# A hybrid attention, recurrence and expert-retrieval block on one core: fewer candidate sums, a gate product shared by two engines, another load order and five score blocks held

## The chip, the cores and the metric

The kernel runs on one core of one Trainium2 chip. The metric is the device time of one execution in microseconds. The time before is the median of three runs, 3784.94 us (3783.61 to 3789.96).

## The reference

One layer over 512 tokens of width 2048. A mixer (forgetting attention with 8 heads beside an RWKV-7 recurrence with 16 heads) is followed by a channel part that retrieves single-neuron experts. A vector `c` modulates both:

```python
mod = silu(c) @ w_ada + b_ada                     # 2048 -> 6 x 2048
h   = rms_norm(x, norm_mix_w) * (1 + sc1) + sh1
x   = x + g1 * (concat(fox(h @ w_in), rwkv(h @ w_in)) @ w_out)
h2  = rms_norm(x, norm_ffn_w) * (1 + sc2) + sh2
# product-key retrieval, 8 heads, 128 x 128 keys, 16384 experts
q = (h2 @ w_query).reshape(T, 8, 2, 128)
s = einsum('thpd,hpkd->thpk', q, sub_keys)
top_s, top_i = top_k(s, 16)                       # per head and key half
cand_s = top_s[:, :, 0, :, None] + top_s[:, :, 1, None, :]   # 16 x 16 sums
best_s, best_pos = top_k(cand_s, 16)
gates = softmax(best_s)
# experts: sum_e gate_e * v_e * gelu(u_e . h2)
x = x + g2 * ffn
```

Both top-16 lists are sorted. A sum of place a in the first and place b in the second list can be among the 16 largest only if (a + 1)(b + 1) is at most 16.

## The kernel before

Activations lie with the model dimension on the partitions, 16 tiles of 128 by 512 tokens. Weights and activations are split into a high and a low part (`split_raw`, L100 and on: ScalarE casts the high part at L103, VectorE or GpSimd subtracts for the low one at L106), and each product is three matmuls (`mm3`, L110 to L112). `Stream` loads weights in halves of 512 KB, splits three halves ahead (`SPLIT`) and hands them to TensorE in one order for the whole kernel.

**Modulation and first projections** (L279 to L385). For the first two of the six modulation vectors, eight rounds of 4 MB of `w_ada` are loaded by `ada_load` (L293) in eight tiles of two rows of blocks each; a tile tag holds `WB` = 11 buffers. In `ada_part` (L300) VectorE multiplies and adds the first eight blocks (`KD`) into two accumulators, while TensorE sums the other eight with `on_pe` in two halves of 256 columns that share one PSUM area, `psx`; VectorE adds each half to an accumulator before the next may be written. `ada_sum` then totals over the partitions, `ada_mod` adds the bias, `first_h` scales two tiles of `x`, and `strm.outer` runs the first seven projections over them on TensorE. The order on VectorE and TensorE is written out by hand here, and three steps of the next round's `ada_part` stand ahead of `ada_mod`.

**Mixer** and its output projection follow, and after them the second norm. They are planned by `Clock`, a small planner in the kernel: each generator yields the TensorE time that it takes and the time after which it is due again, and the planner picks what is emitted next. Outside the parts ordered by hand a scheduler of the framework may still move instructions of an engine.

**Routing** (`route`, L1056). The sixteen query projections `wq` are followed by scores against 128 sub-keys (L1068). For each of four tiles of tokens VectorE takes the 16 largest of 128 (L1073 to L1078: maximum of eight, index search, replacement, maximum, index search). After the second half of a head it builds the 256 sums of a tile with one addition (`cd`, L1088), takes their 16 largest in the same five passes (L1091 to L1096), and finds the two key indices by comparing the high and the low four bits of the position with 0 to 15 (`eq`, L1112; L1123). GpSimd does the low-part subtractions of `wq` meanwhile.

**Gates** (`gates`, L1131). For 320 of the 512 tokens the gates become a dense 128 x 128 matrix a token: a one-hot vector of the first key (`oa`) against one of the second key times the gate (`ob`), multiplied on TensorE (L1186), four tokens a group, eight groups a block of 32 tokens. `oa` is built by VectorE in every second group, by GpSimd (L1164) or ScalarE (L1167, L1168) in the others; `ob` always by VectorE, in four comparisons with a multiplication in the same instruction (L1172). ScalarE copies the result to `gst` (L1188), and each block of 32 tokens is stored to DRAM (`g_d`). Two groups are built ahead, in three buffers.

**Experts.** `scores(e)` (L1038) computes a block of 128 experts for the 320 tokens: 48 matmuls and a Gelu. The first `NB` = 11 blocks are computed ahead of the last stage; `fill2` emits the last `LAST` = 3 of them after the gates. The last stage reads the gates back (`gt`, L1276), weighs the activations (L1278), splits them (L1284, L1285) and combines them with `v`, while the other 192 tokens gather their experts' rows by indirect DMA.

Of the kernel before, what the change touches and what calls it, by code (L numbers as in the profile page):

```python
# [18 lines left out]
P = 128  # L19
# [12 lines left out]
def block_kernel(ctx: ExitStack, tc: tile.TileContext, I: dict, O: dict, dbg=None):  # L32
# [223 lines left out]
    LAST = 3  # L256
# [22 lines left out]
    with ExitStack() as x0:  # L279
        x0.enter_context(tc.manual_schedule(engines={mybir.EngineType.DVE, mybir.EngineType.PE}))  # L280
        p0 = x0.enter_context(tc.tile_pool(name="ph0", bufs=1, reuse_waits="tile"))
        KD, WB = 8, 11
# [10 lines left out]
        def ada_load(jj):  # L293
            w = []
            for a in (4, 5, 6, 7, 0, 1, 2, 3):
                w.append(p0.tile([P, 2, T], F32, tag="wada", name=f"wada{jj}{a}", bufs=WB))
                nc.sync.dma_start(w[-1], I["wada"][jj, :, a * 2:(a + 1) * 2, :])
            return w[4:] + w[:4]

        def ada_part(jj, w, acc):  # L300
# [9 lines left out]
            for k in range(KD):  # L310
                a, wk = acc[k % 2], w[k // 2][:, k % 2, :]
                if k == 3:
                    on_pe(hs[0])
# [4 lines left out]
                if k in (4, 7):  # L318
                    c_ = hs[k // 6]
                    V.tensor_tensor(acc[1][:, c_], acc[1][:, c_], psx, op=ALU.add)  # L320
                    if k == 4:
                        on_pe(hs[1])
                yield
            V.tensor_tensor(acc[0], acc[0], acc[1], op=ALU.add)

# [32 lines left out]
        for k in range(NK):  # L358
            x = xs[k] if k < 2 else p0.tile([P, T], F32, tag=("prd", "acc2")[k % 2], name=f"n1sq{k}", bufs=2)
# [684 lines left out]
    with ExitStack() as rx:  # L1044
# [11 lines left out]
        def route(n, pj, tops):  # L1056
# [8 lines left out]
            yield 0.0, 1.0  # L1065
# [6 lines left out]
            for t in range(NT):  # L1072
                V.max(tv[:, p_, t, 0:8], sc[:, t, :])  # L1073
                V.max_index(ti[:, p_, t, 0:8], tv[:, p_, t, 0:8], sc[:, t, :])
                s2 = px.tile([P, 256], F32, tag="s2", name=f"s2{n}{t}", bufs=2)
                V.match_replace(s2[:, :P], tv[:, p_, t, 0:8], sc[:, t, :], NEG)
                V.max(tv[:, p_, t, 8:16], s2[:, :P])
                V.max_index(ti[:, p_, t, 8:16], tv[:, p_, t, 8:16], s2[:, :P])  # L1078
# [6 lines left out]
            bi = px.tile([P, 3, NT, 16], U32, tag="bi", name=f"bi{h}", bufs=2)  # L1085
            for t in range(NT):
                cd = px.tile([P, 16, 16], F32, tag="cd", name=f"cd{h}{t}", bufs=2)
                V.tensor_tensor(cd, tv[:, 0, t, :, None].to_broadcast([P, 16, 16]),  # L1088
                                tv[:, 1, t, None, :].to_broadcast([P, 16, 16]), op=ALU.add)
                cf = cd.rearrange("p a b -> p (a b)")  # L1090
                V.max(bv[:, t, 0:8], cf)  # L1091
                V.max_index(bi[:, 0, t, 0:8], bv[:, t, 0:8], cf)
                s2 = px.tile([P, 256], F32, tag="s2", name=f"c2{h}{t}", bufs=2)
                V.match_replace(s2, bv[:, t, 0:8], cf, NEG)
                V.max(bv[:, t, 8:16], s2)
                V.max_index(bi[:, 0, t, 8:16], bv[:, t, 8:16], s2)  # L1096
                yield 0.0, ck.dve(2.05)
# [340 lines left out]
```

## Time and profile before

| | |
|---|---|
| median of three runs | 3784.94 us |
| the profiled execution | 3788.3 us |
| its span, first to last instruction | 3786.6 us |
| TensorE busy | 3525.6 us, 93% |
| VectorE busy | 3065.7 us, 81% |
| ScalarE busy | 1247.1 us, 33% |
| GpSimd busy | 1101.4 us, 29% |
| mean granted TensorE clock | 0.962 |

Busy shares over the whole span mix stages with different limits. The stages can be told apart by line: modulation up to some 157 us, mixer and output projection to 1490, second norm and first query projections to 1598, routing to 1823, gates to 1941, the wait for the gates' way through DRAM to 1967, experts to the end. In a timeline the first column is the start, the second the time that the listed instructions last; the distance from one start to the next is the step, which is shorter than the duration where instructions overlap.

### The profile page before, as it was taken

The page shows a single profiled execution, that of the slowest core. Times are in us where ns is not written, and L with a number is a line of the kernel's source. Part 1 is how long each engine was busy: PE and PEld are TensorE (multiplying, and loading weights), DVE is VectorE, ACT ScalarE, POOL GpSimd, SP SyncE. Part 2 cuts the span into 40 slices and gives each one's busy share as a digit, 9 for nine tenths or more (in the row PEclk, how much of TensorE's full clock was granted, in tenths as well). Part 3 has the DMA queues.
Part 4 walks back from the last instruction along what each step waited for, and adds up shares of the span by engine and source line. Part 5 has one row for each costly group of instructions (what it writes and reads, how often), then busy time and mean ns, then how long its engine had stood idle before and what let it go on. Part 6 is the DMA issues. An engine that isn't in the chain of part 4 may idle for free.

```text
span 3786.6 us, 55808 instructions
## 1 busy us (share of the span) xinstructions
PE 3525.6 (93%) x21269; PEld 3127.3 (83%) x21269; DVE 3065.7 (81%) x5314; ACT 1247.1 (33%) x1807; POOL 1101.4 (29%) x692
## 2 busy tenths in 40 slices
PE   6888989999899999998969999999999999999999
PEld 4666766766667778777869999999999999999999
DVE  5687677786875564599978989898989989999996
ACT  3332322423323321323643333333333333333332
POOL 3310110100100000431333444444434444444540
PEclk9888989999989998999989999999999999999999
DMA  8633342433433565222469999999999999999996
GB/s 336 220 105 94 107 119 67 135 93 99 114 113 106 172 211 174 80 81 84 170 247 355 393 384 380 386 389 393 392 379 391 395 383 382 383 387 390 392 386 224
DMA packets 317821, 955.43 MB, mean 252 GB/s; under 512 B 77161, under 2 KB 121449, under 8 KB 266609
## 3 DMA queue, kind: packets, MB, share of 16 engines
q1 hardware_dynamic: 210416, 541.84, 40.0%
q0 software_dynamic: 55296, 402.68, 26.6%
q10 hardware_dynamic: 51840, 7.35, 1.3%
q8 instruction: 167, 2.74, 0.3%
q14 instruction: 102, 0.83, 0.1%
HBM read 916.32 MB, written 35.41 MB: 251 GB/s over the span
## 4 chain that ended last, share of the span: by engine, by line
PE 54%; DVE 16%; DMA 6%; issue 3%; ACT 2%; POOL 0%; ACTq 0%; SPq 0%; DVEq 0%; POOLq 0%
PE po L112 8%; PE po L111 7%; PE po L110 7%; DMA wadl<-wada 3%; DVE rows L1262 2%; DMA u_0raw<-uT 1%; DVE accl L413 1%; DVE ob L1172 1%; PE gp L1186 1%; DVE hl L1285 1%; DVE h2t L1270 1%; DVE pr L636 1%; DVE eq L1112 1%; DVE cd L1088 1%; ACT u_0h L103 1%
## 5 line engine op out<-in xcount | busy, mean ns | idle before, releaser
L1251 POOL DMA_INDIRECT rows<-vn,idx x192 | 401.1, 2089 | 459.5 <-DVE h2t L1270 428.5
L1251 POOL DMA_INDIRECT rows<-un,idx x192 | 363.2, 1892 | 538.9 <-DVE rows L1262 520.3
L1270 DVE SCALAR_TENSOR_TENSOR h2t<-rows,gat,h2t 128x2048 f32<-128x2048 f32 x190 | 445.8, 2346 | 1.3
L1262 DVE SCALAR_TENSOR_TENSOR rows<-rows,h2t 128x2048 f32<-128x2048 f32 x192 | 435.8, 2284 | 0.0
L413 DVE SCALAR_TENSOR_TENSOR accl<-wadl,c,accl 128x256 f32<-128x256 f32 x480 | 245.4, 511 | 106.0 <-DMA wadl<-wada 96.8
L103 ACT CAST u_1h<-u_1raw 128x1024 fp32r<-128x1024 f32 x128 | 134.6, 1051 | 333.2 <-PE po L111 265.0
L103 ACT CAST u_0h<-u_0raw 128x1024 fp32r<-128x1024 f32 x128 | 134.4, 1050 | 297.7 <-DMA u_0raw<-uT 19.0
L1296 DVE TENSOR_TENSOR acc<-acc,po 128x320 f32<-128x320 f32 x240 | 115.5, 481 | 63.5 <-PE po L112 63.4
L106 DVE TENSOR_TENSOR u_1l<-u_1raw,u_1h 128x1024 fp32r<-128x1024 f32 x128 | 155.9, 1218 | 6.6 <-ACT u_1h L103 6.6
L106 DVE TENSOR_TENSOR u_0l<-u_0raw,u_0h 128x1024 fp32r<-128x1024 f32 x128 | 155.9, 1218 | 0.0
L1278 DVE TENSOR_TENSOR at<-at,gt 128x320 f32<-128x320 f32 x128 | 62.1, 489 | 94.1 <-ACT at L1041 83.9
L756 DVE SCALAR_TENSOR_TENSOR st<-st,pend,pu 64x64 f32<-64x64 f32 x240 | 67.0, 279 | 62.8 <-PE pu L752 58.7
L636 DVE TENSOR_TENSOR pr<-zz,msys 128x16 f32<-128x16 f32 (+30 forms) x248 | 105.9, 427 | 3.9
L106 POOL TENSOR_TENSOR wq_0l<-wq_0raw,wq_0h 128x1024 fp32r<-128x1024 f32 x13 | 33.9, 2606 | 241.7 <-ACT wq_0h L103 241.7
L1186 PE MATMUL gp<-ob,oa 128*128 128x128 f32 x640 | 83.9, 281 | 15.8 <-ACT oa L1168 14.3
L1164 POOL TENSOR_SCALAR oa<-iota,selT 128x128 f32<-128x128 f32 x80 | 61.6, 785 | 126.5 <-ACT selT L1150 73.5
L1186 PEld LDWEIGHTS gp<-ob,oa 128*128 128x128 f32 x640 | 77.3, 191 | 21.3 <-ACT oa L1168 16.5
L1172 DVE TENSOR_SCALAR ob<-iota,selT 128x128 f32<-128x128 f32 x320 | 89.2, 346 | 0.0
L743 POOL MEMSET st<- 64x64 f32 x16 | 2.3, 146 | 253.9 <-DVE st L756 253.9
L638 DVE TENSOR_REDUCE zz<-pr 128x8 f32<-128x16 f32 (+30 forms) x248 | 71.4, 288 | 2.5
L103 ACT CAST wF_0h<-wF_0raw 128x1024 fp32r<-128x1024 f32 x32 | 33.6, 1049 | 97.7 <-PE wF43ps L111 13.3
L740 DVE TENSOR_TENSOR uh<-uh,pw 32x128 f32<-32x128 f32 x120 | 34.1, 284 | 37.4 <-PE pw L739 34.8
(4432 smaller groups left out, 12463.9 us busy)
## 6 DMA issues: line engine op xcount, KB each, us to landing
wadl<-wada SPq DMA_DIRECT2D x256, 256.0 KB, 3.0
u_0raw<-uT SPq DMA_DIRECT2D x128, 512.0 KB, 10.0
u_1raw<-uT SPq DMA_DIRECT2D x128, 512.0 KB, 9.7
wada<-wada SPq DMA_DIRECT2D x64, 512.0 KB, 9.0
gt<-g_d SPq DMA_DIRECT2D x32, 640.0 KB, 14.4
g_d<-gst SPq DMA_DIRECT2D x10, 1920.0 KB, 6.6
wF_0raw<-win SPq DMA_DIRECT2D x32, 512.0 KB, 3.8
wF_1raw<-win SPq DMA_DIRECT2D x32, 512.0 KB, 3.6
```

The lines of the kernel that those rows point to most:

```text
L103: S.copy(wh, raw)
L106: eng.tensor_tensor(wl, raw, wh.bitcast(F32), op=ALU.subtract)
L110: PE.matmul(ps, ah, bh, start=first, stop=False)
L111: PE.matmul(ps, ah, bl, start=False, stop=False)
L112: PE.matmul(ps, al, bh, start=False, stop=last)
L413: V.scalar_tensor_tensor(acc, w[:, k, :], c16[:, a + k:a + k + 1], acc, op0=ALU.mult, op1=ALU.add)
L636: V.tensor_tensor(pr[:, :, :m], zz[:, s_:, :].rearrange("p t j -> p j t"), msys[:, s_:s_ + 1, s_:].to_broadcast([P, 8, m]), op=ALU.mult)
L1172: V.tensor_scalar(ob[:, u, :], iota, selT[:, 1, t0 + u:t0 + u + 1], selT[:, 2, t0 + u:t0 + u + 1], op0=ALU.is_equal, op1=ALU.mult)
L1186: PE.matmul(b0.rearrange("p (j t) -> p t j", t=4)[:, u, :], oa[:, u, :], ob[:, u, :], start=True, stop=True)
L1251: G.indirect_dma_start(out=b_, out_offset=None, in_=I["vn" if side else "un"], in_offset=bass.IndirectOffsetOnAxis(ap=idx[i][:, c_:c_ + 1] ...
L1262: V.scalar_tensor_tensor(b_, b_, 1.0, h, op0=ALU.mult, op1=ALU.mult, accum_out=dot[i][:, c_:c_ + 1])
L1270: V.scalar_tensor_tensor(h, b_, g[:, c_:c_ + 1], h, op0=ALU.mult, op1=ALU.add)
```

## The change

The routing builds 112 sums a head and tile: the first four places of the first list with all sixteen of the second (64 sums), and places 4 to 15 with the first four of the second (48 sums), with two additions for all four tiles. Passes are 112 wide. The position is decoded for both parts and joined with three more operations; the tiles for it have one buffer. The gates build `ob` in five of eight groups with one two-input comparison on VectorE, and ScalarE multiplies the gate in; ScalarE no longer builds `oa`, GpSimd does in three of eight groups. Three groups are built ahead, in four buffers. The modulation's tiles load in order, in twelve buffers; VectorE does all its multiply-adds and the join of the accumulators before it adds the first half from TensorE, and both halves go to the joined accumulator. Five score blocks are emitted after the gates instead of three.

```diff
-    LAST = 3
+    LAST = 5
-        KD, WB = 8, 11
+        KD, WB = 8, 12
         def ada_load(jj):
-            for a in (4, 5, 6, 7, 0, 1, 2, 3):
+            for a in range(8):
...
-            return w[4:] + w[:4]
+            return w
             for k in range(KD):
                 a, wk = acc[k % 2], w[k // 2][:, k % 2, :]
-                if k == 3:
-                    on_pe(hs[0])
...
-                if k in (4, 7):
-                    c_ = hs[k // 6]
-                    V.tensor_tensor(acc[1][:, c_], acc[1][:, c_], psx, op=ALU.add)
-                    if k == 4:
-                        on_pe(hs[1])
+                if k == KD - 2:
+                    on_pe(hs[0])
                 yield
             V.tensor_tensor(acc[0], acc[0], acc[1], op=ALU.add)
+            V.tensor_tensor(acc[0][:, hs[0]], acc[0][:, hs[0]], psx, op=ALU.add)
+            on_pe(hs[1])
+            V.tensor_tensor(acc[0][:, hs[1]], acc[0][:, hs[1]], psx, op=ALU.add)
...
-            x = xs[k] if k < 2 else p0.tile([P, T], F32, tag=("prd", "acc2")[k % 2], name=f"n1sq{k}", bufs=2)
+            x = xs[k] if k < 2 else p0.tile([P, T], F32, tag="prd", name=f"n1sq{k}", bufs=3)
...
             S.copy(qs, pj)
-            yield 0.0, 1.0
+            yield 0.0, 3.0
...
-            bi = px.tile([P, 3, NT, 16], U32, tag="bi", name=f"bi{h}", bufs=2)
+            bi = px.tile([P, 5, NT, 16], U32, tag="bi", name=f"bi{h}", bufs=1)
+            cd = px.tile([P, NT, 112], F32, tag="cd", name=f"cd{h}", bufs=1)
+            for u, (a0, a1, nb) in enumerate(((0, 4, 16), (4, 16, 4))):
+                na = a1 - a0
+                V.tensor_tensor(cd[:, :, u * 64:u * 64 + na * nb].rearrange("p t (a b) -> p t a b", b=nb),
+                                tv[:, 0, :, a0:a1, None].to_broadcast([P, NT, na, nb]),
+                                tv[:, 1, :, None, 0:nb].to_broadcast([P, NT, na, nb]), op=ALU.add)
             for t in range(NT):
-                cd = px.tile([P, 16, 16], F32, tag="cd", name=f"cd{h}{t}", bufs=2)
-                V.tensor_tensor(cd, tv[:, 0, t, :, None].to_broadcast([P, 16, 16]),
-                                tv[:, 1, t, None, :].to_broadcast([P, 16, 16]), op=ALU.add)
...
-                yield 0.0, ck.dve(2.05)
+                yield 0.0, ck.dve(1.35)
...
-            V.tensor_copy(bf, bi[:, 1:3].rearrange("p a t s -> p a (t s)"))
+            V.tensor_scalar(bi[:, 3], bi[:, 0], 124, 6, op0=ALU.bitwise_and, op1=ALU.logical_shift_left)
+            V.tensor_scalar(bi[:, 4], bi[:, 0], 3, 8, op0=ALU.bitwise_and, op1=ALU.logical_shift_left)
+            bf = px.tile([P, 5, NT * 16], F32, tag="bf", name=f"bf{h}", bufs=1)
+            V.tensor_copy(bf, bi.rearrange("p a t s -> p a (t s)"))
+            V.scalar_tensor_tensor(bf[:, 1, :], bf[:, 3, :], -3072.0, bf[:, 1, :], op0=ALU.add, op1=ALU.max)
+            V.scalar_tensor_tensor(bf[:, 2, :], bf[:, 0, :], 64.0, bf[:, 2, :], op0=ALU.is_lt, op1=ALU.mult)
+            V.tensor_tensor(bf[:, 2, :], bf[:, 2, :], bf[:, 4, :], op=ALU.max)
...
-            yield 0.0, ck.dve(4.4) + 0.5
+            yield 0.0, ck.dve(5.4) + 0.5
...
-                oa = pg.tile([P, 4, P], F32, tag="oa", name=f"oa{t0}", bufs=3)
-                ob = pg.tile([P, 4, P], F32, tag="ob", name=f"ob{t0}", bufs=3)
-                if q % 4 == 1:
+                oa = pg.tile([P, 4, P], F32, tag="oa", name=f"oa{t0}", bufs=4)
+                ob = pg.tile([P, 4, P], F32, tag="ob", name=f"ob{t0}", bufs=4)
+                if q in (1, 4, 6):
                     for u in range(4):
                         G.tensor_scalar(oa[:, u, :], iota, selT[:, 0, t0 + u:t0 + u + 1], None, op0=ALU.is_equal)
-                elif q % 4 == 3:
-                    for u in range(4):
-                        S.activation(oa[:, u, :], iota, AF.Abs, bias=selT[:, 0, t0 + u:t0 + u + 1], scale=-1.0)
-                    S.activation(oa, oa, AF.Relu, bias=cvals[:, 2:3], scale=-1.0)
                 else:
                     V.tensor_tensor(oa, io4, quad(0, t0), op=ALU.is_equal)
-                for u in range(4):
-                    V.tensor_scalar(ob[:, u, :], iota, selT[:, 1, t0 + u:t0 + u + 1],
-                                    selT[:, 2, t0 + u:t0 + u + 1], op0=ALU.is_equal, op1=ALU.mult)
+                if q in (0, 3, 7):
+                    for u in range(4):
+                        V.tensor_scalar(ob[:, u, :], iota, selT[:, 1, t0 + u:t0 + u + 1],
+                                        selT[:, 2, t0 + u:t0 + u + 1], op0=ALU.is_equal, op1=ALU.mult)
+                else:
+                    V.tensor_tensor(ob, io4, quad(1, t0), op=ALU.is_equal)
+                    for u in range(4):
+                        S.activation(ob[:, u, :], ob[:, u, :], AF.Copy, scale=selT[:, 2, t0 + u:t0 + u + 1])
...
-            ahead = [onehots(0), onehots(1)]
+            ahead = [onehots(0), onehots(1), onehots(2)]
```

## Rows read from the trace of the kernel before

**Rows 1.** Stages: us; busy us (instructions) of five engines; granted clock; DMA share; GB/s
```profile
core 0: us, PE busy (x) PEld busy (x) DVE busy (x) ACT busy (x) POOL busy (x), PEclk, DMA share, GB/s
0.00:157.00 157.00, 108.75 (x595) 77.77 (x595) 81.11 (x157) 43.10 (x61) 54.54 (x37) 0.91 0.78 300
...
1598.00:1823.00 225.00, 202.15 (x1018) 175.53 (x1017) 223.49 (x924) 64.86 (x88) 55.98 (x25) 0.94 0.26 88
1823.00:1941.00 118.00, 102.04 (x789) 96.34 (x788) 118.00 (x370) 86.54 (x190) 61.75 (x78) 1.00 0.46 182
1941.00:1967.00 26.00, 8.92 (x62) 8.66 (x60) 4.01 (x7) 4.45 (x7) 4.40 (x4) 0.73 1.03 377
1967.00:3786.00 1819.00, 1763.74 (x11824) 1745.66 (x11824) 1646.71 (x1608) 598.75 (x733) 757.36 (x380) 0.99 0.97 375
```

**Rows 2.** Timeline of TensorE, modulation: start, duration, engine, line, tiles [idle before]
```profile
44.48 1.07 PE L306 MATMUL psm<-wada,c 128*32 128x256 f32 x16
46.09 1.07 PE L306 MATMUL psm<-wada,c 128*32 128x256 f32 x16 [0.54 <-DVE acc L320]
49.45 1.05 PE L331 MATMUL psm<-ones,acc 128*128 128x1 f32 x8 [2.29 <-DVE acc L324]
...
105.34 0.63 PE L111 MATMUL wR00ps<-hl,win_6h 128*128 128x512 f32 x1
```

**Rows 3.** Timeline of VectorE in the round of rows 2
```profile
45.62 0.42 DVE L320 TENSOR_TENSOR acc<-acc,psm 128x256 f32<-128x256 f32 x1 [4.53 <-PE psm L306]
...
48.71 0.69 DVE L324 TENSOR_TENSOR acc<-acc,acc 128x512 f32<-128x512 f32 x1
```

**Rows 4.** Timeline of VectorE, routing
```profile
1789.93 0.29 DVE L1073 MAX8 tv<-scs 128x8 f32<-128x128 f32 x1
1790.13 0.28 DVE L1077 MAX8 tv<-s 128x8 f32<-128x128 f32 x1
...
1804.27 0.42 DVE L1091 MAX8 bv<-cd 128x8 f32<-128x256 f32 x1
1804.61 0.41 DVE L1088 TENSOR_TENSOR cd<-tv 128x256 f32<-128x256 f32 x1
...
1814.02 0.19 DVE L1099 TENSOR_SCALAR bi<-bi 128x64 uint32<-128x64 uint32 x1
1814.12 0.21 DVE L1107 TENSOR_TENSOR sel<-bv 128x64 f32<-128x64 f32 x1
```

**Rows 5.** Group of instructions, VectorE, routing: count | busy us, mean ns | idle before
```profile
L1088 DVE TENSOR_TENSOR cd<-tv 128x256 f32<-128x256 f32 x32 | 22.5, 706 | 0.0
```

**Rows 6.** Timeline of VectorE, gates
```profile
1926.89 0.67 DVE L1170 TENSOR_TENSOR oa<-iota,selT 128x512 f32<-128x512 f32 x1
1927.50 2.31 DVE L1172 TENSOR_SCALAR ob<-iota,selT 128x128 f32<-128x128 f32 x8
```

**Rows 7.** Timeline of GpSimd, gates: a group of four, and its first alone
```profile
1926.66 3.06 POOL L1164 TENSOR_SCALAR oa<-iota,selT 128x128 f32<-128x128 f32 x4 [2.44 <-PE gp L1186]
...
1926.66 1.32 POOL L1164 TENSOR_SCALAR oa<-iota,selT 128x128 f32<-128x128 f32 x1 [2.44 <-PE gp L1186]
```

**Rows 8.** Timeline of ScalarE, gates
```profile
1930.35 0.69 ACT L1167 ACTIVATE oa<-iota,selT 128x128 f32<-128x128 f32 x2
1930.95 0.57 ACT L1188 COPY gst<-gp 128x512 f32<-128x512 f32 x1
1931.41 0.70 ACT L1167 ACTIVATE oa<-iota,selT 128x128 f32<-128x128 f32 x2
```

**Rows 9.** Timeline of TensorE, gates (eight records are one group of four tokens)
```profile
1927.78 4.20 PE L1186 MATMUL gp<-ob,oa 128*128 128x128 f32 x32 [1.29 <-ACT oa L1168]
```

**Rows 10.** Timeline of VectorE, routing: two subtractions in a row
```profile
1735.16 4.55 DVE L1112 TENSOR_TENSOR eq<-tf,bf 128x1024 f32<-128x1024 f32 x2
```

**Rows 11.** Timeline of GpSimd in the stretch of rows 10
```profile
1736.01 2.62 POOL L106 TENSOR_TENSOR wq_1l<-wq_1raw,wq_1h 128x1024 fp32r<-128x1024 f32 x1 [7.37 <-ACT wq_1h L103]
```

**Rows 12.** One tile's instructions: ns min/median/max, first and last start us
```profile
L110 PE MATMUL u8ps<-hh,u_0h x8: 309/309/393, 1846.5 to 1854.7; 128*128 128x320 f32 x8
```

**Rows 13.** Waits from 1945 to 2000: us in total, times, longest
```profile
PE po L110 <- ACT hh L1284: 17.1, 1, 17.1
```

More of the change, by code (lines that the diff above doesn't have):

```diff
@@ L1074, in route @@
                 V.max_index(ti[:, p_, t, 0:8], tv[:, p_, t, 0:8], sc[:, t, :])
[L1075 to L1078, printed above, removed]
+                s2 = px.tile([P, P], F32, tag="s2", name=f"s2{n}{t}", bufs=2)
+                V.match_replace(s2, tv[:, p_, t, 0:8], sc[:, t, :], NEG)
+                V.max(tv[:, p_, t, 8:16], s2)
+                V.max_index(ti[:, p_, t, 8:16], tv[:, p_, t, 8:16], s2)
                 yield 0.0, ck.dve(1.05)
@@ L1086, in route @@
             for t in range(NT):
-                cd = px.tile([P, 16, 16], F32, tag="cd", name=f"cd{h}{t}", bufs=2)
-                V.tensor_tensor(cd, tv[:, 0, t, :, None].to_broadcast([P, 16, 16]),
-                                tv[:, 1, t, None, :].to_broadcast([P, 16, 16]), op=ALU.add)
-                cf = cd.rearrange("p a b -> p (a b)")
+                cf = cd[:, t, :]
                 V.max(bv[:, t, 0:8], cf)
                 V.max_index(bi[:, 0, t, 0:8], bv[:, t, 0:8], cf)
-                s2 = px.tile([P, 256], F32, tag="s2", name=f"c2{h}{t}", bufs=2)
@@ L1094, in route @@
-                V.match_replace(s2, bv[:, t, 0:8], cf, NEG)
-                V.max(bv[:, t, 8:16], s2)
-                V.max_index(bi[:, 0, t, 8:16], bv[:, t, 8:16], s2)
-                yield 0.0, ck.dve(2.05)
+                s2 = px.tile([P, P], F32, tag="s2", name=f"c2{h}{t}", bufs=2)
+                V.match_replace(s2[:, :112], bv[:, t, 0:8], cf, NEG)
+                V.max(bv[:, t, 8:16], s2[:, :112])
+                V.max_index(bi[:, 0, t, 8:16], bv[:, t, 8:16], s2[:, :112])
+                yield 0.0, ck.dve(1.35)
@@ L1098, in route @@
             V.tensor_scalar(bi[:, 1], bi[:, 0], 240, 4, op0=ALU.bitwise_and, op1=ALU.logical_shift_left)
             V.tensor_scalar(bi[:, 2], bi[:, 0], 15, 8, op0=ALU.bitwise_and, op1=ALU.logical_shift_left)
-            bf = px.tile([P, 2, NT * 16], F32, tag="bf", name=f"bf{h}", bufs=2)
-            V.tensor_copy(bf, bi[:, 1:3].rearrange("p a t s -> p a (t s)"))
+            V.tensor_scalar(bi[:, 3], bi[:, 0], 124, 6, op0=ALU.bitwise_and, op1=ALU.logical_shift_left)
+            V.tensor_scalar(bi[:, 4], bi[:, 0], 3, 8, op0=ALU.bitwise_and, op1=ALU.logical_shift_left)
@@ L1112, in route @@
                 V.tensor_tensor(eq, tf[:, q_, :, None, :].to_broadcast([P, NT, 16, 16]),
-                                bf[:, q_, :].rearrange("p (t s) -> p t s", s=16)[:, :, :, None].to_broadcast(
+                                bf[:, 1 + q_, :].rearrange("p (t s) -> p t s", s=16)[:, :, :, None].to_broadcast(
                                     [P, NT, 16, 16]), op=ALU.subtract)
@@ L1191, in gates @@
                     nc.sync.dma_start(g_d[tg, :, GB:], gst[:, GB:])
-                if x + 2 < NTG * nq:
-                    ahead.append(onehots(x + 2))
+                if x + 3 < NTG * nq:
+                    ahead.append(onehots(x + 3))
                 yield 0.85, 0.65
```

## Prediction

> **What bounds the kernel now.** I read the table of stages first, then the timeline of one engine after the other inside each stage that the change touches, and the table of waits last. The table of stages [rows 1] splits the span where the kind of work changes. Up to 157 us the modulation columns are summed while the first projections run; no engine is full there, so the length must come from waits. From 1598 to 1823 VectorE is busy 223.5 of 225 us: it sets the pace of the routing. From 1823 to 1941 it is busy all of 118 us: it sets the pace of the gates too, with TensorE at 102, ScalarE at 87 and GpSimd at 62. In the last 1819 us TensorE is busy 97% and the DMA engines 97%; the change touches nothing there, so I leave that stage as long as it is, and the mixer between 157 and 1490 as well. What is gained before either of them moves it earlier as a whole.
>
> **Modulation.** TensorE shows the wait of a round [rows 2]: sums of the first half at 44.48, of the second at 46.09, and the column totals only at 49.45, after a wait of 2.29 us for VectorE. A round's path from the first sums to the totals is 4.97 us. VectorE shows why [rows 3]: it takes the first half 1.14 us after those sums start (45.62), then still has three multiply-adds, the second half's addition and the join of its two accumulators (48.71) to do. The change puts all multiply-adds and the join ahead of the first addition, where they run beside the long TensorE stretch of projections that ends at 44.48. What is left behind: 1.61 us to the second sums (as now), 1.14 us until VectorE can take them, and about 0.47 us for a half-width addition and the hand-over (the full-width join took 0.74 from its start to the totals): 3.22 us, so 1.75 us less. There are seven such rounds: 12 us. In the first round the tiles of TensorE now come last, but VectorE's come 4 tiles earlier and its whole sum is then done when the last tile lands; I give this 1 us, between -1 and 2. The twelfth buffer frees the next round's first four loads one round earlier, so the order of loads costs nothing; without that cover VectorE would wait some 2 us a round, the 1.75 again. On SP's queue the projection weights stand behind these loads, whose last now waits for the fourth multiply-add pair; that is still in the same round, and each weight is wanted a round later. Sum: **-13 us**. Bounds: -7 if only half the overlap comes, -27 if the matmuls at half speed that follow these waits (0.63 us apiece [rows 2], and some ten in a round) vanish too. I take the near end, since a shorter wait is still a wait. The norm's third buffer in place of four costs nothing: VectorE's addition there takes longer than ScalarE's square.
>
> **Routing.** VectorE's own start-to-start steps are the prices [rows 4]. A maximum over 128 takes 0.20 us, over 256 0.34: 1.05 ns an element, so 0.18 at 112. Each token tile has five such passes over the sums (two maxima, two index searches, one replacement): 5 x 0.155 = 0.76 us, in 8 heads x 4 tiles 24.3 us. The 32 additions that build the sums step like a maximum of their width, 0.33 apiece (10.6); now 16 with 256 and 192 sums, 0.30 on average (4.8): 5.8 less. Their mean duration was 706 ns [rows 5] against 0.41 us for an undisturbed one [rows 4], which is waiting behind GpSimd's subtractions; I leave those 9 us as they are, as the new small two-input operations can meet them as well. Added a head: two integer operations at 0.10 [rows 4], a conversion of 320 in place of 128 (some 0.2 more), three 64-wide operations, bounded by 0.10 (the integer one's step) and 0.21 (a full duration), 0.14 taken: 0.8 us, 6.6 in all. Net 23. The score matmuls are placed 2 us later after their copy, which delays the first by about two projection steps, 1.4 us. Sum: **-22 us**, between -10 and -26. TensorE doesn't take over: it is busy 202 of the 225 us [rows 1], a score block of some 7 us less now that six stand ahead of the gates in place of eight, so 195 against the 203 that VectorE needs.
>
> **Gates.** Count per eight groups of four tokens. VectorE: a one-hot by two-input comparison steps 0.61 us, four one-input multiply-comparisons 1.03 to 1.15 a group, the more the longer GpSimd works beside them [rows 6]. Before: 4 x 0.61 + 8 x 1.03 = 10.7 (four groups took 4.20 and a wait of 1.29, 5.5 [rows 9]). After: five first and five second comparisons, 10 x 0.61, and three groups at 1.03: 9.2. ScalarE: two 128-wide activations step 0.60, a copy 0.46 [rows 8]; after: 8 copies and 20 multiplications, 9.7. TensorE: 4.20 for four groups [rows 9], 8.4. Its first multiplication of a group now waits for VectorE's comparison, and behind it in ScalarE's queue stands the copy for which TensorE's next PSUM bank waits; three groups built ahead, 3 x 1.1 us, cover that, and without them some 0.7 us a group would show. GpSimd: 12 comparisons instead of 8. One alone takes 0.58, but the one that began at 1926.66 took 1.32 [rows 7], because VectorE's two-input comparison ran from 1926.89 [rows 6]: the two don't read together. In VectorE's stretch there are now ten of these instead of four. The nearest row on who gives way is in the routing: two 1024-wide subtractions of VectorE lasted 4.55 us together [rows 10] with a GpSimd subtraction from 1736.01 [rows 11] between them: GpSimd gets in at the boundary, and VectorE then waits for it. If each of seven GpSimd comparisons caught among two-input ones holds VectorE for what is left of 0.58 after the 0.23 us that passed before it was blocked, at most 0.35 and about 0.25, VectorE needs 9.2 + 1.7 = 10.9. Ten times that and 3 us to start: 112 against 118 now, **-6 us**. Bounds: 100 if no one is held and ScalarE sets the pace (-18), 135 if GpSimd is shut out as in [rows 7] all through a run: 10 x 0.61 + 12 x 0.59 = 13.2 a time (+17). I take the hand-over, as the rows with several two-input operations in a row show it.
> The Trainium skill, SBUF — State Buffer, § SBUF: two separate sides, calls the pair of ports that VectorE and GpSimd share an exclusive lock that an operation with two SBUF inputs keeps for the whole instruction, while the other blocks; the 1.32 us and the 4.55 us agree, and the rule speaks against doubling such operations here. By it alone the gates come out near the 135 us above. ScalarE: Activation LUTs, § Rules for kernel authors, sends a multiplication to VectorE and not to ScalarE; by that nothing would be gained here, and the gates would stay at 118.
>
> **Five blocks held.** The hold is not what the trace has: u8, the first of three held ones, ran from 1846.5, in the middle of the gates [rows 12], because three half-blocks of weights are split ahead. After the gates the gate tile goes out and back, 26 us in which TensorE was busy 8.9 us with 62 matmuls [rows 1] and waited 17.1 us [rows 13]. A block is 48 matmuls, 7 us. With five held, one and a half can again run inside, so 3.5 x 7 = 25 us follow the gates where the way takes 26. The blocks fill what was idle, and what they leave inside the gates is TensorE time that nothing waited for. Their weights must now be loaded beside the gate tile: **+2 us**, between -1 and +9 (all five behind: 35 instead of 26).
>
> **Sum.** -13 - 22 - 6 + 2 = -39. The profiled execution took 3788.3 us (span 3786.6): 3749. The median of the runs shown is 3784.9, 3.4 lower: **3746**.
>
> **Rivals.**
> Gates without contention: ScalarE sets 9.7 a time, 100 us: 3734. For it: the ports clash in the routing was with GpSimd's long two-input subtractions, here it has one input. Against: the 1.32.
> GpSimd shut out: gates 135 us, 3769. For it: runs of four and five two-input comparisons; against: the hand-over seen in [rows 10, 11].
> All five blocks behind the gates: 7 us more, 3753. Against: [rows 12].
> The routing's chain exposed: where one head runs alone, each pass waits for the one before, 0.28 (the duration) instead of 0.20 [rows 4]; 160 passes at 0.08 are 13 us: 3759. Against: VectorE interleaves two heads now and had no idle time.
> Slower than before: TensorE at its lower level in the gates. Place: the 80 groups; 4.20 us for four become 8.4, 171 us with the start, 59 more than forecast: 3805, 20 slower than now. It decides once the gaps between groups grow to those after which the rounds of the first stage ran at half level (2.3 us [rows 2]); for it, fewer blocks are there to fill; against, gaps of 1.29 us in every 5.5 went with a granted clock of 1.00 [rows 1, 9], and the new gaps are shorter pieces.
> That the change doesn't do what it says holds for the hold of the blocks only, as costed.
>
> **How the numbers follow.** Forecast 0.48, no contention 0.16, shut out 0.13, all behind 0.09, chain exposed 0.08, lower level 0.06. The range takes in the first five and, at its low end, part of the half-speed matmuls of the first stage: 3724 to 3772. A measurement of this kernel tells 0.2% (7.6 us) from no change. Each of the first five alone ends more than that below 3785; only shut out, chain exposed and all behind at once (39 - 23 - 13 - 7 = 4 us below) end within it, for which I keep 0.05 out of their chances; slower is the lower level and what I don't see, 0.06. Faster: 0.89.
>
> **What would show it.** In the modulation: totals 3.2 us after the first sums, no wait of 2.29 before them, the stage's end near 144. In the routing: passes at 0.18, VectorE still without idle time, its end 35 us earlier than 1823. In the gates: comparisons of VectorE stretched beyond 0.68 where GpSimd works, GpSimd's beyond 1.3, the period of eight groups near 10.9. After them: TensorE's wait of 17.1 down to a few us. It is wrong if VectorE shows idle time in the routing, if a comparison of GpSimd takes several times 0.58, or if the granted clock in the gates leaves 1.00.

## The result and the profile after

The changed kernel takes 0.9929 of the time of the kernel before (95% interval 0.9913 to 0.9946): some 27 us less, between 20 and 33, where 39 were forecast (a median of 3746 us). Its profiled execution took 3763.0 us (span 3761.3, before 3786.6), 25.3 less by the span. The medians of the comparison are 3762.4 and 3787.5 us.

The stages of after, in the order and with the columns of [rows 1]:

```profile
core 0: us, PE busy (x) PEld busy (x) DVE busy (x) ACT busy (x) POOL busy (x), PEclk, DMA share, GB/s
0.00:136.00 136.00, 95.91 (x562) 67.64 (x563) 101.32 (x155) 42.71 (x61) 60.22 (x36) 0.95 0.89 339
...
1576.00:1793.00 217.00, 195.56 (x1007) 169.05 (x1006) 213.96 (x950) 62.32 (x87) 56.72 (x25) 0.96 0.27 90
1793.00:1905.00 112.00, 94.63 (x695) 83.84 (x693) 97.92 (x222) 97.94 (x280) 108.21 (x116) 1.00 0.43 175
1905.00:1939.00 34.00, 29.79 (x168) 28.73 (x169) 14.16 (x20) 13.34 (x22) 4.32 (x4) 0.85 0.96 347
1939.00:3761.00 1822.00, 1766.06 (x11826) 1746.57 (x11825) 1644.30 (x1601) 597.54 (x730) 755.41 (x380) 0.99 0.96 375
```

Cut at the same events in every trace (first matmul of the next projection, `wR10ps`; first matmul of `wq4ps`; first gate matmul; last copy to `gst`; first matmul of `po`), all profiled executions of this study stand side by side. The sums of a row are the spans.

| kernel | modulation | mixer, second norm | routing | gates | way to `po` | experts |
|---|---|---|---|---|---|---|
| before | 176.3 | 1418.4 | 229.6 | 115.7 | 27.0 | 1819.6 |
| after | 154.9 | 1417.6 | 221.5 | 110.7 | 34.4 | 1822.2 |
| e1_mod | 155.6 | 1422.2 | 229.5 | 115.7 | 26.5 | 1830.7 |
| e2_route | 174.8 | 1421.5 | 222.1 | 117.9 | 25.7 | 1822.6 |
| e3_gates | 175.2 | 1424.4 | 227.3 | 112.6 | 26.6 | 1833.0 |
| e4_hold | 173.3 | 1414.4 | 229.8 | 112.1 | 29.2 | 1831.0 |
| e5_last4 | 154.4 | 1429.8 | 223.0 | 110.9 | 28.2 | 1833.6 |
| e6_gp2 | 154.5 | 1421.1 | 221.6 | 110.2 | 28.8 | 1827.7 |
| e7_quarter | 154.4 | 1424.4 | 205.6 | 111.6 | 34.5 | 1816.3 |
| e8_exp | 155.6 | 1415.6 | 216.4 | 111.2 | 28.3 | 1822.4 |
| e9_fill | 192.9 | 1414.0 | 229.7 | 115.5 | 26.8 | 1827.7 |
| e11_quarter_before | 175.3 | 1418.1 | 219.3 | 115.8 | 26.0 | 1821.4 |
| e12_one_op | 154.5 | 1419.8 | 222.2 | 113.6 | 34.1 | 1823.2 |
| e13_all | 155.3 | 1427.8 | 201.8 | 108.1 | 26.7 | 1828.4 |

Each row is one execution. Two columns belong to no edit: mixer and experts move by up to 17 us between executions (1414 to 1430, 1816 to 1834). The other four repeat within some 3 us where nothing was edited. An effect of 5 us is therefore read from its stage; the ratio alone would not show it. By stage the change is -21.4 (modulation), -0.8, -8.1 (routing), -5.0 (gates), +7.4 (way), +2.6: -25.3. The prediction said -13, 0, -22, -6, +2, 0.

**Modulation.** TensorE in a round of after; compare [rows 2]:

```profile
78.05 1.07 PE L306 MATMUL psm<-wada,c 128*32 128x256 f32 x16
79.66 1.07 PE L306 MATMUL psm<-wada,c 128*32 128x256 f32 x16 [0.55 <-DVE acc L320]
81.30 1.05 PE L329 MATMUL psm<-ones,acc 128*128 128x1 f32 x8 [0.57 <-DVE acc L322]
82.21 0.48 PE L110 MATMUL wR00ps<-hh,win_4h 128*128 128x512 f32 x1
```

First sums to totals: 3.25 us where 3.22 were predicted and 4.97 stood before. The idle 2.29 us is 0.57. And the granted clock of a round is 1.00 instead of 0.90 from the third round on. The third round of before, then the second and third of after:

```profile
62.71:79.92 17.21, 14.38 (x84) 10.68 (x83) 8.05 (x17) 4.56 (x6) 7.38 (x5) 0.90 0.78 305
```
```profile
45.09:63.81 18.72, 14.96 (x83) 10.41 (x83) 12.01 (x17) 5.50 (x7) 10.98 (x5) 0.91 1.03 409
63.81:78.05 14.24, 13.11 (x84) 9.46 (x83) 11.80 (x17) 4.56 (x6) 6.79 (x5) 1.00 0.87 317
```

The third round lasts 14.24 us where that of before lasts 17.21: 1.7 of the difference is the shorter path, and the rest lies in TensorE, busy 1.3 us less at the higher clock. Up to 63.81 us after is no earlier than before (62.71): the DMA engines are full there (1.03, 409 GB/s), and TensorE waits for a weight. The matmuls behind that wait, and the first of them at half speed:

```profile
59.04 0.50 PE L112 MATMUL wR02ps<-hh,win_2l 128*128 128x512 f32 x1 [2.57 <-POOL win_2l L106]
...
60.40 0.63 PE L111 MATMUL wL1ps<-hl,win_2h 128*128 128x512 f32 x1
```

All of the 21 us comes from the rounds behind.

**Routing.** VectorE's groups that the change moved (count | busy us, mean ns | idle before). Two of before, beside the one in [rows 5]:

```profile
L1112 DVE TENSOR_TENSOR eq<-tf,bf 128x1024 f32<-128x1024 f32 x16 | 23.2, 1487 | 0.0
...
L1121 DVE TENSOR_TENSOR sel<-sel,gs 128x64 f32<-128x64 f32 x8 | 3.3, 410 | 0.0
```

The groups of after:

```profile
L1121 DVE TENSOR_TENSOR eq<-tf,bf 128x1024 f32<-128x1024 f32 x16 | 26.8, 1677 | 0.0
L1110 DVE TENSOR_TENSOR bf<-bf 128x64 f32<-128x64 f32 x8 | 10.4, 1296 | 0.0
L1130 DVE TENSOR_TENSOR sel<-sel,gs 128x64 f32<-128x64 f32 x8 | 9.3, 1163 | 0.0
...
L1107 DVE CAST bf<-bi 128x320 f32<-128x320 uint32 x8 | 4.2, 528 | 0.1
L1089 DVE TENSOR_TENSOR cd<-tv 128x192 f32<-128x192 f32 x8 | 4.1, 518 | 0.0
L1089 DVE TENSOR_TENSOR cd<-tv 128x256 f32<-128x256 f32 x8 | 3.2, 405 | 0.0
```

The additions that build the sums fell from 22.5 to 7.3 us, 9 more than predicted. Two operations on 64 elements, each some 0.2 us long when undisturbed, took 19.7: `bf`, which joins the two decoded positions and is new, and `sel`, the gate product. `eq` grew by 3.6. Their place in one head, VectorE and then GpSimd:

```profile
1671.05 1.22 DVE L1121 TENSOR_TENSOR eq<-tf,bf 128x1024 f32<-128x1024 f32 x1
1672.19 2.37 DVE L1110 TENSOR_TENSOR bf<-bf 128x64 f32<-128x64 f32 x1
1674.48 2.40 DVE L1130 TENSOR_TENSOR sel<-sel,gs 128x64 f32<-128x64 f32 x1
1676.80 3.42 DVE L1121 TENSOR_TENSOR eq<-tf,bf 128x1024 f32<-128x1024 f32 x1
```
```profile
1671.27 3.20 POOL L106 TENSOR_TENSOR wq_1l<-wq_1raw,wq_1h 128x1024 fp32r<-128x1024 f32 x1 [19.66 <-ACT wq_1h L103]
1674.44 2.35 POOL L106 TENSOR_TENSOR wq_0l<-wq_0raw,wq_0h 128x1024 fp32r<-128x1024 f32 x1
1676.76 2.38 POOL L106 TENSOR_TENSOR wq_1l<-wq_1raw,wq_1h 128x1024 fp32r<-128x1024 f32 x1
```

Three subtractions of GpSimd stand in a row. `bf` ends with the first (1674.5), `sel` with the second (1676.8), and the second `eq` ends 1.1 us, its own length, after the third (1679.1): 7 us lost in one head.

**Gates.** GpSimd is busy 108.2 us (below the min, median and max of a comparison in ns; they were 597, 601 and 1734 before), VectorE waits for buffers, and TensorE now waits for GpSimd (waiter, releaser, us in total, times, longest):

```profile
L1173 POOL TENSOR_SCALAR oa<-iota,selT x120: 594/1104/1848, 1789.7 to 1902.9; 128x128 f32<-128x128 f32 x120
```
```profile
PE gp L1196 <- POOL oa L1173: 14.4, 23, 0.8
DVE oa L1175 <- PE gp L1196: 9.8, 13, 1.0
```

**The way to the last stage.** ScalarE, then TensorE, at the end of the gates; then two half-blocks, with the min, median and max of a matmul in ns, first and last start:

```profile
1904.06 1.26 ACT L1198 COPY gst<-gp 128x512 f32<-128x512 f32 x2 [0.36 <-PE gp L1196]
1905.21 1.05 ACT L103 CAST u_1h<-u_1raw 128x1024 fp32r<-128x1024 f32 x1
```
```profile
1906.31 0.42 PE L110 MATMUL u7ps<-hh,u_1h 128*128 128x320 f32 x1 [1.62 <-ACT u_1h L103]
```
```profile
L110 PE MATMUL u7ps<-hh,u_1h x8: 417/468/468, 1906.3 to 1912.8; 128*128 128x320 f32 x8
...
L110 PE MATMUL u10ps<-hh,u_1h x8: 309/426/468, 1933.2 to 1938.7; 128*128 128x320 f32 x8
```

Three and a half blocks follow the gates, as predicted, but they take 32.8 us and not 25. The cast for the first half-block stands behind the last copies on ScalarE; TensorE has idled 1.6 us by then, and this half takes 7 us, at 468 ns a matmul instead of 309. The last half-block waits 1.3 us for its late weights and their cast, and about half of it is slow again. The first `po` matmul waits for them, no longer for the gate tile as in [rows 13].

### The profile page after: what moved, and what is told of

It reads as the page before. It is cut to its first block, busy times and chain, and to the rows that moved or that the text cites. A ratio compares the mean times of both kernels' runs of the same rounds, so it can differ in the third digit from the quotient of the medians.

```text
span 3761.3 us, 55894 instructions
## 1 busy us (share of the span) xinstructions
PE 3520.8 (94%) x21269; PEld 3119.1 (83%) x21269; DVE 3058.6 (81%) x5198; ACT 1263.3 (34%) x1907; POOL 1157.9 (31%) x732
## 4 chain that ended last, share of the span: by engine, by line
PE 51%; DVE 15%; DMA 8%; issue 3%; POOL 3%; ACT 1%; SPq 0%; DVEq 0%; ACTq 0%; POOLq 0%
PE po L112 7%; PE po L111 7%; PE po L110 7%; DMA wadl<-wada 3%; DMA u_0raw<-uT 3%; POOL oa L1173 2%; DVE rows L1272 2%; DVE accl L411 1%; DMA u_1raw<-uT 1%; DVE hl L1295 1%; DVE h2t L1280 1%; DVE eq L1121 1%; ACT u_0h L103 1%; DVE pr L634 1%; PE n2ss L226 0%
## 5 line engine op out<-in xcount | busy, mean ns | idle before, releaser
L103 ACT CAST u_0h<-u_0raw 128x1024 fp32r<-128x1024 f32 x128 | 134.4, 1050 | 308.1 <-DMA u_0raw<-uT 26.8
L1306 DVE TENSOR_TENSOR acc<-acc,po 128x320 f32<-128x320 f32 x240 | 115.5, 481 | 64.2 <-PE po L112 64.2
L1173 POOL TENSOR_SCALAR oa<-iota,selT 128x128 f32<-128x128 f32 x120 | 110.7, 942 | 63.2 <-ACT selT L1159 60.1
L1196 PEld LDWEIGHTS gp<-ob,oa 128*128 128x128 f32 x640 | 78.5, 191 | 27.7 <-POOL oa L1173 25.7
L103 ACT CAST wF_1h<-wF_1raw 128x1024 fp32r<-128x1024 f32 x32 | 33.5, 1046 | 94.9 <-DMA zb<-zd 12.0
L1183 ACT ACTIVATE ob<-ob,selT 128x128 f32<-128x128 f32 x200 | 64.1, 399 | 0.0
```

Of the source, the lines that this page charges most:

```text
L103: S.copy(wh, raw)
L1173: G.tensor_scalar(oa[:, u, :], iota, selT[:, 0, t0 + u:t0 + u + 1], None, op0=ALU.is_equal)
L1196: PE.matmul(b0.rearrange("p (j t) -> p t j", t=4)[:, u, :], oa[:, u, :], ob[:, u, :], start=True, stop=True)
```

## The experiments

All ratios are times against the kernel before, with the 95% interval; the changed kernel's own is 0.9929.

**One part each, on the kernel before.** The hunks of the diff were taken alone; of each the first line or two stand here. The rest of e1 is `ada_load`, `ada_part` and `n1sq`, of e2 all from `s2` to the delay behind `eq`, of e3 all of `ob` and `ahead`.

```diff
-        KD, WB = 8, 11
+        KD, WB = 8, 12
...
```

> The modulation's part alone on the kernel before (load order, twelve buffers, the order of additions). Theory, from the changed kernel's trace: from the third round on a round's path is 3.2 us instead of 5.0 and the granted clock no longer falls, so rounds of 17.2 to 19.7 us become 14.2 to 15.1; the first two rounds gain nothing, since the DMA engines are full there. The stage ends near 136 us instead of 157, and all of it is kept: the time is 19 to 22 us less. Rival, the prediction's term: 13 us less, half-speed matmuls remain behind the shorter wait.

Ratio 0.9945 (0.9926 to 0.9964). The stage ends 20.7 us earlier, and a round there repeats the path (75.79, 77.40, 79.04) and the clock of 1.00. So the whole 21 us belongs to this part; the 13 are refuted. Its three pieces (order of loads, twelfth buffer, order of additions) were not run apart.

```diff
-            yield 0.0, 1.0
+            yield 0.0, 3.0
...
+            cd = px.tile([P, NT, 112], F32, tag="cd", name=f"cd{h}", bufs=1)
...
```

> The routing's part alone on the kernel before (112 sums, decoding, score matmuls 2 us later). Theory: the passes give 24 us as predicted, but VectorE's short two-input operations now stand behind GpSimd's subtractions, two or three of which follow each other, so 12 to 15 us more waiting comes back: the routing gains 7 to 11 us, and so does the time. Rival, the prediction's term: the waits stay as they were, 22 us less.

Ratio 0.9990 (0.9976 to 1.0004), not told apart from no change; routing -7.5 us, gates +2.2. The two groups are there as in after:

```profile
L1112 DVE TENSOR_TENSOR bf<-bf 128x64 f32<-128x64 f32 x8 | 10.4, 1297 | 0.0
L1132 DVE TENSOR_TENSOR sel<-sel,gs 128x64 f32<-128x64 f32 x8 | 9.3, 1167 | 0.0
```

The loss lies inside the routing's own part, not in its meeting with the others.

```diff
-                if q % 4 == 1:
+                if q in (1, 4, 6):
...
```

> The gates' part alone on the kernel before, three blocks held as before. Theory: GpSimd sets the pace with 12 comparisons of some 0.94 us in eight groups, 11.2 us, whatever VectorE still has free: the stretch from the first gate matmul to the last copy is 110 to 114 us instead of 115.7, 2 to 6 us less time. Rival 1, the prediction's: VectorE is held by GpSimd; with 8 us of weight splits in this stretch it would need 118 and more, no gain. Rival 2, nobody is held: 101 to 104 us, 12 to 15 us less.

Ratio 0.9990 (0.9977 to 1.0004), again not told apart from no change; gates 112.6 us (-3.1), inside the theory's range, but not far outside what the stage does unedited (115.5 to 117.9). Rival 2 is out. So is rival 1: VectorE idles 9.1 us here, so it isn't the full engine.

```diff
-    LAST = 3
+    LAST = 5
```

> Five score blocks held instead of three, alone on the kernel before. Theory: two blocks' splits (six or seven of 1.15 us) leave VectorE in the gates, which it bounds here, so the gates end 6 to 8 us earlier; after them three and a half blocks instead of one and a half follow, 34 us instead of 26; the time moves by -1 to +3 us. Rival 1: the gates don't shorten and the time is 8 us more. Rival 2, the prediction's: the blocks fit into the 26 us, and the time would be up to 7 us less, or the same if the gates don't shorten.

Ratio 1.0004 (0.9989 to 1.0019): gates -3.6, way +2.2. VectorE splits (subtracts for the low part of) three weight halves before the last copy of the gates where six stood before; 3 x 1.21 us is the 3.6, and this term the prediction had not counted. Alone, the way costs the +2 that was predicted.

**Around the changed kernel.**

```diff
-    LAST = 5
+    LAST = 4
```

> The changed kernel with four score blocks held instead of five. In the changed kernel three and a half blocks follow the gates, and 34.4 us pass to the first matmul of the last stage. Theory: two and a half blocks need some 20 to 24 us, the gate tile's way through DRAM of 26 us then ends last: 26 to 28 us, 6 to 8 less; of that up to 2.3 us comes back in the routing or the gates, where VectorE splits the block's weights. The time is 4 to 8 us less than the changed kernel's. Rival: the stretch is set by the loads behind the gate tile and stays at 32 to 35 us.

Ratio 0.9911 (0.9889 to 0.9934). The way is 28.2 us instead of 34.4, routing +1.5, gates +0.2: 4.5 us by stage, the low end of the theory. Three blocks follow the gates here, not two and a half: of the four held ones one ran inside. The first half of them again waits 1.62 us for its cast and takes 468 ns a matmul.

```diff
-                if q in (1, 4, 6):
+                if q in (1, 5):
```

> The changed kernel with GpSimd building the first one-hots of two groups in eight instead of three; VectorE builds six. Theory: GpSimd set the pace with 12 comparisons of 0.94 us; with 8 of them it needs at most 8.8 us a time, and VectorE with eleven two-input comparisons at 0.62 and twelve one-input ones at 0.27 needs 10.1: the stretch of the gates is 102 to 106 us instead of 110.7, and TensorE waits for VectorE instead of GpSimd. Rival, VectorE is held by GpSimd: it was full already, and the stretch gets longer, 113 to 118 us.

Ratio 0.9935 (0.9915 to 0.9956). The theory falls: the stretch stays at 110.2. GpSimd is busy 87.0 us and a comparison's median is still 1100 ns; VectorE is at 103.1, TensorE at 99.7, ScalarE at 99.3, and TensorE's waits split between GpSimd (4.6) and ScalarE (4.3). The rival's slowing isn't there either. What GpSimd gave up went into TensorE: the second half of block u7 ran inside, and the way fell by 5.6 us to 28.8. Three engines are at 90% or more here and GpSimd at 79%; what bounds the stretch now is open.

```diff
-        eng.tensor_tensor(wl, raw, wh.bitcast(F32), op=ALU.subtract)
+        whf = wh.bitcast(F32)
+        m = HK // 4 if tag[:2] == "wq" else HK
+        for i in range(0, HK, m):
+            eng.tensor_tensor(wl[:, i:i + m], raw[:, i:i + m], whf[:, i:i + m], op=ALU.subtract)
```

> The changed kernel with GpSimd's subtraction for a query weight half (128 x 1024) cut into four of 128 x 256. Theory: a short two-input operation of VectorE waits for the end of the one GpSimd instruction that runs, 2.4 us now and some 0.65 then; the join of the position (mean 1296 ns) and the gate product (1163 ns) fall below 600 ns, and the routing stage of 221.5 us ends 8 to 14 us earlier. Rival 1, dependences within VectorE make these operations long: no change. Rival 2, GpSimd takes the port for as long as it has work, whatever the length of its instructions: no change or longer, since four instructions cost more than one.

Ratio 0.9878 (0.9855 to 0.9901), routing 205.6 us, -15.9:

```profile
L1113 DVE TENSOR_TENSOR bf<-bf 128x64 f32<-128x64 f32 x8 | 4.4, 555 | 0.0
L1133 DVE TENSOR_TENSOR sel<-sel,gs 128x64 f32<-128x64 f32 x8 | 4.1, 515 | 0.0
...
L1110 DVE CAST bf<-bi 128x320 f32<-128x320 uint32 x8 | 2.6, 320 | 0.1
```

The same 22 subtractions in pieces of some 0.74 us, the same dependences, and the two groups fall from 19.7 to 8.5 us. The wait lasts as long as what is left of the GpSimd instruction that runs. Both rivals are out. The conversion ahead of the join, which has one input, fell as well, from 528 to 320 ns: such an operation can meet GpSimd too. VectorE is no longer alone at the limit: it is busy 198.1 of the 205.6 us, TensorE 197.2.

```diff
-            S.activation(gx, gx, AF.Exp)
             yield 0.0, ck.dve(5.4) + 0.5
+            S.activation(gx, gx, AF.Exp)
+            yield 0.0, 1.0
```

> The changed kernel with the exponential of a head emitted a step later (after the planner's time for the two subtractions instead of before it). Theory: ScalarE waits for VectorE in front of the exponential, 84.8 us in all and up to 22.6 at once, and the casts of the query weights stand behind it, so GpSimd's subtractions come two and three in a row; emitted later, the longest wait falls below 15 us, the subtractions come singly, and the routing stage of 221.5 us ends 3 to 8 us earlier. Rival: VectorE waits for the same number of subtractions wherever they lie, no change within 2 us.

Ratio 0.9907 (0.9887 to 0.9927), routing -5.1. ScalarE's longest wait for VectorE fell from 22.6 to 11.0 us, yet subtractions still come in threes (1651.47, 1654.18, 1656.53), and `bf` still takes 1280 ns. The size fits, the mechanism only in part: the wait that went is that of the gate product, which this edit emits a step later.

```profile
L1131 DVE TENSOR_TENSOR sel<-sel,gs 128x64 f32<-128x64 f32 x8 | 1.6, 202 | 0.0
```

It took 9.3 us in after. Of these 7.7 us, 3.2 came back in two other two-input groups, an addition (3.2 to 5.0) and a step of the join (1.7 to 3.1). Block u7 ran inside the gates here (1802 to 1830), and the way is 28.3.

> The kernel before with GpSimd's subtraction for a query weight half cut into four. Theory: before, VectorE waits some 10 us for GpSimd in the routing (9 of them in the 32 additions of 706 ns that build the sums) against 23 us in the changed kernel; so the routing stage of 229.6 us gains 6 to 10 us here, against 15.9 us in the changed kernel, and the additions fall to 420 to 500 ns. Rival: the shorter subtractions help in another way (weights earlier for TensorE), and the gain is the same 16 us.

The edit of e7 on the kernel before. Ratio 0.9982 (0.9964 to 0.9999), routing -10.3 us:

```profile
L1091 DVE TENSOR_TENSOR cd<-tv 128x256 f32<-128x256 f32 x32 | 14.8, 464 | 0.0
L1124 DVE TENSOR_TENSOR sel<-sel,gs 128x64 f32<-128x64 f32 x8 | 3.3, 415 | 0.0
```

The theory holds, just above its upper edge; the rival's 16 us did not come. With quarters the change's routing gains 13.7 us (219.3 to 205.6), without 8.1. Of what is still missing to 22, VectorE's groups show 3.2 in `eq` (23.1 against 19.9), 2.8 in `bf` beyond 0.2 us an operation and 0.8 in `sel`: waits that the quarters shorten but do not end.

**The clock in the modulation**, on the kernel before:

```diff
+                        if jj:
+                            fill_pe(22)
...
+        def fill_pe(n):
+            for i in range(n):
+                PE.matmul(pmb[:, 288:512], hh[:, 0, :P], hh[:, 0, :224], start=True, stop=True)
```

> The kernel before with 22 matmuls of 224 columns put on TensorE behind the second half's sums of each modulation round but the first (into columns of the bank that nothing reads); they only fill the wait for VectorE. Theory: it is the idle 2.3 us that lowers the granted clock behind it, and eight to eleven matmuls of a round at 0.43 instead of 0.21 us cost 1.7 to 2.4 us; with the wait filled the clock stays at 1.00 and the rounds of 17.2 to 19.7 us become 15.5 to 17, 10 to 16 us less at the end of the stage, though no step of the path is shorter. Rival: the clock falls for another reason (the sums on 32 columns, the loads), the matmuls stay at 0.63 us and the stage stays within 3 us or gets longer by the fillers.

Ratio 1.0030 (1.0013 to 1.0048), the stage 16.6 us longer.

```profile
48.20 2.71 PE L330 MATMUL psm<-hh 128*128 128x224 f32 x22
52.15 1.05 PE L337 MATMUL psm<-ones,acc 128*128 128x1 f32 x8 [1.24 <-DVE acc L326]
...
54.19 0.63 PE L111 MATMUL wR01ps<-hl,win_1h 128*128 128x512 f32 x1
```
```profile
50.95 0.42 DVE L320 TENSOR_TENSOR acc<-acc,psm 128x256 f32<-128x256 f32 x1 [1.70 <-PE psm L330]
```

The edit missed its aim: VectorE's second addition waited for the fillers, which write the same tile, so the path grew from 4.97 to 6.57 us and a wait of 1.24 was left. Matmuls still went to 0.63 us behind it. That the wait of 2.3 us alone lowers the clock isn't shown. Shown is that the clock stays at 1.00 in the rounds of after with 0.55 and 0.57 idle, and that the second round of after, with the same two waits, has 1.00 up to 55 us and 0.81 from there on, where the wait of 2.57 us lies.

**One GpSimd instruction a group**, on the changed kernel:

```diff
-                    for u in range(4):
-                        G.tensor_scalar(oa[:, u, :], iota, selT[:, 0, t0 + u:t0 + u + 1], None, op0=ALU.is_equal)
+                    G.tensor_tensor(oa, io4, quad(0, t0), op=ALU.subtract)
```

> The changed kernel with GpSimd's four one-input comparisons of a group replaced by one two-input operation on 128 x 512, a difference instead of a comparison: the gates' values are left out of the computation, its work is not. Theory: GpSimd waits for a two-input operation of VectorE once an instruction, so 30 waits remain of 120, its busy time in the gates falls from 108 to 45 to 60 us, but VectorE now waits up to the 1.2 us of such an operation, 30 times; the stretch of 110.7 us ends up between 102 and 116 us, decided by whether a comparison of VectorE is found that lasts over 1.2 us at each. Rival 1, VectorE never waits: 100 to 104 us, no comparison beyond 0.8 us. Rival 2: each of the 30 holds VectorE for its full length, 97 + 36, 125 to 135 us.

Ratio 0.9935 (0.9913 to 0.9958), gates 113.6 us, 2.9 longer than after. The groups of GpSimd, then of VectorE:

```profile
L1172 POOL TENSOR_TENSOR oa<-iota,selT 128x512 f32<-128x512 f32 x29 | 70.2, 2419 | 44.3 <-PE gp L1195 42.1 <-DVE ob L1180 1.4 <-DVE ob L1177 0.8
```
```profile
L1177 DVE TENSOR_SCALAR ob<-iota,selT 128x128 f32<-128x128 f32 x116 | 53.6, 520 | 0.0
L1180 DVE TENSOR_TENSOR ob<-iota,selT 128x512 f32<-128x512 f32 x50 | 33.0, 678 | 0.0
```

Within the theory's range, but not at its place: VectorE's two-input comparisons aren't held (678 ns), and GpSimd is busy 70.2 us where 45 to 60 were expected. GpSimd's operation, 1.04 us at its shortest, waits through a run of them (2.4 us on average) and then holds the one-input ones (520 ns instead of 350).

**All four edits together**, e5 to e8:

> The changed kernel with the four edits together: GpSimd's weight subtractions of the routing in quarters, the exponential a step later, four blocks held, GpSimd in two groups of eight in the gates. Theory: the parts add up stage by stage: the first stage as in the changed kernel (155 us), routing 201 to 206 us instead of 221.5, gates 109 to 112, the way to the last stage 26 to 29 instead of 34.4. Against the kernel before that is 21 + 25 + 5 - 1, some 48 to 53 us, a ratio of 0.986 to 0.988. Rival: the routing's end then falls to TensorE, busy 176 of 184 us there with the quarters, and the later exponential and the extra block give nothing: 0.988 to 0.990.

Ratio 0.9865 (0.9843 to 0.9887), 51 us less than before. Routing 201.8, gates 108.1, way 26.7: the parts add up. The rival's ratio (0.988 to 0.990) touches the interval; by stage it is out, since routing is 3.8 us and the way 7.8 us shorter than in e7. It beats both kernels: its interval ends below that of the changed kernel.

## Why the prediction was right or wrong

- **Modulation, -13; measured -21.** Mechanism and path were right to 0.03 us. The term was mis-sized at the choice of its end: I kept the half-speed matmuls "since a shorter wait is still a wait", and they went. The -27 had them all gone in seven rounds; the first two gained nothing, since loads bind there: TensorE waited 2.57 us for a weight in the second (0.70 before), where I had put the weights' place behind the loads at nothing.
- **Routing, -22; measured -8.** The step that failed is "I leave those 9 us as they are". The passes came as priced (0.263 us long instead of 0.409, 160 times: 23), and VectorE stayed full. But the waits behind GpSimd are not a property of the 32 additions. They go to whichever two-input operation comes next, and the change put a short one between the two long subtractions (`eq`, `bf`, `eq`), where GpSimd gets in. [rows 10, 11] show that entry, and I used them for the gates only. Against my terms the additions gave 9 more, but `bf` took 9 more, `sel` 6 and `eq` 4; smaller groups took the rest. e7 and e11 show the wait itself. The score delay cost 2.0 us at the start (1572.5 to 1578.4, before 1594.7 to 1598.6), not 1.4.
- **Gates, -6; measured -5, for other reasons.** I held VectorE for GpSimd, to 10.9 us a time. VectorE's two-input comparisons lasted 0.71 us instead of 0.68; GpSimd was held (0.95 a comparison on average, 11.4 a time, and up to 1.85, over three times 0.58: one of my signs of being wrong). And part of the gain is not the gates' own: e3 gave 3.1, the splits that the hold moved away 3.6 (e4). Nearly one number by two ways: the sum alone would have confirmed the wrong one. The Trainium skill, SBUF — State Buffer, § SBUF: two separate sides, says that whichever operation starts first keeps the shared ports for its whole instruction. The routing agrees: in e7 the waits shrink with the instruction. The 1.32 us that I counted for it is no clean case: GpSimd's comparison is recorded as starting 0.23 us before VectorE's [rows 6, 7], and still it waited, while VectorE's took its usual 0.67. The 135 us that I drew from it for the gates did not come. ScalarE: Activation LUTs, § Rules for kernel authors, in the same notes, the Trainium skill, sends multiplications to VectorE. I had drawn from it that nothing would be gained here; e3, which has them on ScalarE beside another change on GpSimd, is 3.1 us shorter there.
- **Five blocks, +2; measured +7.4**, near the far bound of +9. The count was right: one and a half blocks inside, three and a half behind. The step that failed is their price, 7 us a block: one half-block out of seven and about half of another ran at the lower clock, behind waits of 1 to 2 us for a cast. In e6 and e8 the first of these halves ran inside the gates, and the way was 28.8 and 28.3, though u8's first half was slow in its place, behind a wait of 2.0 us; the last half ran at 309 ns. e4 alone had the +2.2. That the wait for the cast causes the lower clock was not tested by itself. I also left out what the hold takes from VectorE inside the gates.
- **The sum** fell inside the range by luck, since the errors had opposite signs: -8, +14, +1 and +5, with +2 from mixer and experts. Of the rivals, none describes what happened: TensorE stayed at 1.00 in the gates, VectorE idled 3 of 217 us in the routing, the price of "all five behind" came without its cause, and the cause of "GpSimd shut out" came in part (0.95 us a comparison), without its price.

## What to carry to other kernels

Where VectorE and GpSimd clash, a wait belongs to the pair of neighbours and not to the instruction that shows it: remove the instruction, and look which two-input operation comes next while GpSimd has work queued. Cutting GpSimd's instruction into four pieces was worth more here than shortening VectorE's work (10.3 us alone, e11, against 7.5, e2), because a wait lasts no longer than the piece. And an engine's queue order can decide whether held-back work fits the gap meant for it: look up what its first step stands behind.

## What the runs showed of the hardware that I had not expected

A two-input operation of 64 elements on VectorE took up to 2.4 us behind one GpSimd subtraction. In the gates the clash went one way: GpSimd's comparisons rose from a median of 0.60 to 1.10 us while VectorE's two-input ones rose by 0.03. With a two-input operation on GpSimd (e12), VectorE's one-input comparisons were held instead, 0.52 us against 0.35, and the two-input ones not at all. Why GpSimd gets in between two-input operations in the routing and not within a run of them in the gates is open.
